# Who issues the copies that begin the sums of the MLP's weights: the load queue, job by job, or GpSimd, several jobs interleaved

## The chip, the cores and the metric

The kernel runs on 1 core of one Trainium2 chip. The metric is the device time of one execution, in microseconds; the number given for a kernel is the median of several runs. The profile is one execution more, taken by the hardware profiler. "Load queue" is SyncE's DMA queue (SP). ScalarE (ACT) and GpSimd (POOL) have a queue each as well.

## The reference, cut to what matters

One layer of a decoder over 2048 tokens of width 1024, all in float32: retention and a pooling mixer, cross-attention into 256 memory tokens, then a gated MLP with a short causal convolution. Two parts matter here: the cross-attention, whose key side starts from the *normalised* memory, and the MLP.

```python
mem_n = rmsnorm(mem, mem_norm_g)
...
q = (h @ wq).reshape(B, S, XA_HEADS, XA_HEAD_DIM)
k, v = jnp.split(mem_n @ wkv, 2, axis=-1)
...
a = h @ w_up                      # 1024 -> 2 x 2816
c = conv_w[0] * a2 + conv_w[1] * a1 + conv_w[2] * a + conv_b
gate, val = jnp.split(c, 2, axis=-1)
return (jax.nn.silu(gate) * val) @ w_down
```

## The kernel before, in words

**Arithmetic.** Each float32 operand is split into a high part that fits TensorE's fast format and a low part, and each product is three matmuls (high by high, high by low, low by high: lines 241, 242, 243, in `passes`). ScalarE makes the high parts, VectorE the low parts (lines 233 and 216).

**The start (`folded_weights`, and `load_x_wide` beside it).** The 16 projections of the memory (`project(n)`, `wkv[n]`, 24 matmuls of 128x256 each) run on the memory without its norm, and the first eight results are multiplied by the norm's factors as they leave PSUM. The factors come from `memory_norm`: ScalarE squares the two halves of the memory (L389), GpSimd adds the squares in five `tensor_tensor` instructions (L216 on POOL), TensorE sums over partitions (L317, tile `aux3`), VectorE takes the inverse root, TensorE spreads it over the partitions (L341, tile `aux9`), ScalarE copies it out (L346). PSUM has five buffers for products (pool `mmp`), so the first five projections (tiles mm1, mm2, mm10, mm11, mm12) can be computed before one has left; the sixth (mm13) needs a buffer back. The memory's two raw tiles lie in arena `Z` and are given back once GpSimd has added them; the loads of x and of the value weights (L540, L659) take the places in `Z` in turn.

**The weights' sums.** The MLP multiplies 2x2 blocks with seven products in place of eight, and for that needs four sums of blocks of each weight: with blocks a11, a12, a21, a22 they are d2 = a21 + a22, d0 = a11 + a21, d1 = a11 + d2 and d3 = a12 + d1. `weight_sums` makes them from DRAM to DRAM, without any engine: four plain copies begin the sums (one block each), then four DMAs with `accum_op=add` finish them. There are 34 jobs, 22 for `w_up` into `Ud` and 12 for `w_dn` into `Dd`; a block is 256 KB (192 KB in four of the jobs). Before the change the copies are issued by SP (L917) and held with `issue_after` behind the last load of a tile that the program has fetched; the accumulating DMAs are issued by POOL (L919, L920, L923, L926). Only GpSimd's queue can accumulate. The sums are read from 1,126 us on, for the MLP.

**What sets the order.** `weight_sums` is a generator kept in `under[0]`; the program takes a step of it now and then (in `unit`, between quarters of a projection, and in `attention`, `pace` steps for each of 16 tiles of rows, `pace` being 1 in the first block of rows and 2 in the second). Whatever is left runs ahead of the MLP. The written order isn't the final one: a scheduler places the instructions of the five engines, by a timeline of its own, and moves an instruction ahead of the place where it was written when its operands allow it. In the finished program each engine goes through its own list strictly in order and waits at an instruction until its semaphores are there. The DMAs of POOL share eight semaphores in turn, so from the ninth on each waits for the one issued eight before it; those of SP and ACT share eight likewise.

Of the kernel before, what the change touches and what calls it, by code (L numbers as in the profile page):

```python
# [12 lines left out]
ALU = mybir.AluOpType  # L13
# [106 lines left out]
def trunk(ctx, tc, xT, memT, pos, w_qkgu, w_v, wkv, wqT, wo, wout_r, wout_p, poolT, w_up, w_dn, vecs, consts, outT):  # L120
    nc = tc.nc
    pe, act, dve, pool, sp = nc.tensor, nc.scalar, nc.vector, nc.gpsimd, nc.sync
# [15 lines left out]
    def new_z(dtype):  # L138
        return Arena(cp.tile([P, 8 * T + 4 * EDGE], dtype, tag="Z", name=nm("Z")), 0, 8, T)
# [58 lines left out]
    def mmps():  # L198
        return mmp.tile([P, SUB], F32, tag="mm", name=nm("mm"))
# [6 lines left out]
    def aux():  # L206
        if both[0] and next(turns_) % 3 == 2:
            return single()
        return auxp.tile([P, SUB], F32, tag="aux", name=nm("aux"))

    def small(n=4):
        t = smp.tile([P, 8], F32, tag="sm", name=nm("sm"))
        return t[:, :n]

    def tt(eng, out, a, b, op):
        return eng.tensor_tensor(out=out, in0=a, in1=b, op=op)  # L216

    def ts(eng, out, a, s1, op0, s2=None, op1=None):
        if op1 is None:
            eng.tensor_scalar(out=out, in0=a, scalar1=s1, scalar2=None, op0=op0)  # L220
        else:
            eng.tensor_scalar(out=out, in0=a, scalar1=s1, scalar2=s2, op0=op0, op1=op1)
# [7 lines left out]
    def split(src, hi, lo, g=None):  # L230

        if g is None:
            act.activation(hi, src, AF.Copy)  # L233
            tt(dve, lo, src, hi.bitcast(F32), ALU.subtract)
        else:
            act.activation(hi, src, AF.Identity, scale=g)
            stt(lo, src, g, hi.bitcast(F32), ALU.mult, ALU.subtract)

    def passes(ps, lhs, rhs, start, stop, more=False):
        (lh, ll), (rh, rl) = lhs, rhs  # L240
        pe.matmul(ps, lh, rh, start=start, stop=False, skip_group_check=more)  # L241
        pe.matmul(ps, lh, rl, start=False, stop=False, skip_group_check=more)  # L242
        latest[0] = pe.matmul(ps, ll, rh, start=False, stop=stop, skip_group_check=more)  # L243

    def new_raw():
        r = raws.take()
        r.free()
        return r.f
# [6 lines left out]
    def pairs(raw):  # L255

        out = []
        for h in range(2):
            r = raw[h] if isinstance(raw, list) else raw[:, h * SUB : (h + 1) * SUB]
            pr = new_pair()  # L260
            split(r, pr[:, 0], pr[:, 1])
            out.append(pr)
        return out
# [15 lines left out]
    behind, under, fetched = [iter(())], [iter(())], [None]  # L279
# [544 lines left out]
    def attention(sums, beside, pace):  # L824


        scl, nscl = (smp.tile([P, 8], F32, tag="scl", name=nm("scl"), bufs=2) for _ in range(2))
        room = B.take(2 * KT)
        third = [Region(B, room.first + KT * i, KT) for i in range(2)] + [new_z(F32R).take(KT)]
        prob = [third[1], third[0]]  # L830

        def load_m(hp):

            out = mw[hp]
            for kp in range(KT // 2):
                raw = new_raw()
                fetched[0] = sp.dma_start(raw.rearrange("p (k n) -> p k n", k=2), Md[hp, 2 * kp : 2 * kp + 2].rearrange("k p n -> p k n"))
                if hp == 0 and kp == 0:

                    out += [(pr[:, 0], pr[:, 1]) for pr in pairs(raw)]  # L840
                    yield
                    continue
                for i in range(2):
                    u = third[2 * hp].r[:, (2 * kp + i) * T : (2 * kp + i + 1) * T]
                    split(raw[:, i * SUB : (i + 1) * SUB], u[:, :SUB], u[:, SUB:])
                    out.append((u[:, :SUB], u[:, SUB:]))
                yield

        def turn(pt, t, e):
            tp = aux()  # L850
            for j in range(4):
                pe.transpose(tp[:, j * P : (j + 1) * P], e.f[:, j * P : (j + 1) * P], ident)  # L852
            pt4 = pt.r.rearrange("p (i k t) -> p i k t", i=2, t=T)[:, :, :, t * P : (t + 1) * P]
            turned.append(act.activation(pt4[:, 0], tp.rearrange("p (k t) -> p k t", k=4), AF.Copy))
            tt(dve, pt4[:, 1], tp.rearrange("p (k t) -> p k t", k=4), pt4[:, 0].bitcast(F32), ALU.subtract)
            e.free()

        turned.clear()
        mw = [[], []]
        for _ in load_m(0):  # L860
            pass
        more_m = load_m(1)
        late = []
        for i in range(2 * KT):
            hp, t = divmod(i, KT)
            ps = mmps()
            for k in range(KT):
                x2 = [X[:, 2 * k + j, t * P : (t + 1) * P] for j in range(2)]
                passes(ps, x2, mw[hp][k], k == 0, k == KT - 1)
            if i == 0:  # L870
                rn, _, _ = norm_tables(sums, wide=False)
                ts(dve, scl, rn, 1.0 / 16.0, ALU.mult)
                ts(dve, nscl, rn, -1.0 / 16.0, ALU.mult)
            mx, sm = small(2), small(2)
            dve.reduce_max(out=mx, in_=ps.rearrange("p (h m) -> p h m", h=2), axis=AX.X)
            ts(dve, mx, mx, nscl[:, t : t + 1], ALU.mult)
            e = TT.take()
            for j in range(2):
                act.activation(e.f[:, j * NMEM : (j + 1) * NMEM], ps[:, j * NMEM : (j + 1) * NMEM], AF.Exp,
                               bias=mx[:, j : j + 1], scale=scl[:, t : t + 1], accum_out=sm[:, j : j + 1])  # L880
            dve.reciprocal(sm, sm)
            for j in range(2):
                ej = e.f[:, j * NMEM : (j + 1) * NMEM]
                ts(dve, ej, ej, sm[:, j : j + 1], ALU.mult)
            if len(late) == 2:
                turn(*late.pop(0))
            late.append((prob[hp], t, e))
            for _ in range(pace):
                next(under[0], None)
            if i < KT - 2:  # L890
                next(more_m, None)
            else:
                for _ in range(pace):
                    next(beside, None)

        def end():
            for one in late:
                yield turn(*one)

        return prob, end()  # L900


    def block(w, g, h, k0, n):

        return w[g][:, k0 + h * n : k0 + (h + 1) * n].rearrange("p k c -> p (k c)")

    def weight_sums():

        jobs = [((w_up[f], w_up[f + NF]), 0, 4, Ud[f]) for f in range(NF)]
        for at, (k0, n) in enumerate(ROUNDS):  # L910
            jobs += [((w_dn[2 * j], w_dn[2 * j + 1]), k0, n, Dd[at, j]) for j in range(KT // 2)]
        for w, k0, n, to, in jobs:
            a11, a12, a21, a22 = (block(w, i // 2, i % 2, k0, n) for i in range(4))
            d = [to[i][:, : n * P] for i in range(4)]
            with tc.issue_after(fetched[0].ins):
                for i, a in ((2, a21), (0, a11), (1, a11), (3, a12)):
                    sp.dma_start(d[i], a)  # L917
            yield
            pool.dma_start(d[2], a22, accum_op=ALU.add, max_dma_last_dim=2048)  # L919
            pool.dma_start(d[0], a21, accum_op=ALU.add, max_dma_last_dim=2048)  # L920
            yield
            yield
            pool.dma_start(d[1], d[2], accum_op=ALU.add, max_dma_last_dim=2048)  # L923
            yield
            yield
            pool.dma_start(d[3], d[1], accum_op=ALU.add, max_dma_last_dim=2048)  # L926

    class Round:

# [409 lines left out]
    pending, later, sums, Y, fetches, firsts = [], [], [], [], [], []  # L1339
# [113 lines left out]
    def norm_tables(s_acc, wide=True, late=False):  # L1453

        rn = rows_norm(s_acc)
        rb, last = [], None
        if wide:
            rb = [TT.take() for _ in range(NS)]
            last = spread(rn, [r.f[:, :SUB] for r in rb], late=late)
        return rn, rb, last  # L1460
# [68 lines left out]
    normed = norm_tables(room[:1])  # L1529
    wv.append(value_weights(3, Z.take()))  # L1530
    under[0] = weight_sums()
    for b in range(NB):

# [49 lines left out]

        beside = tables() if b + 1 < NB else first_tiles(own)
        prob, behind[0] = attention(xs, beside, b + 1)
        for _ in beside:
            pass
# [181 lines left out]
```

## Time and profile before

| | |
|---|---|
| Time, 3 runs | 2470.78 us median (2470.77 to 2472.31) |
| The profiled execution | 2470.94 us, of which its span 2469.2 us |
| Granted TensorE clock, mean | 0.996 |
| Busy share: PE, PEld, DVE, ACT, POOL | 98%, 82%, 69%, 49%, 7% |
| DMA queues, MB: SP's, POOL's, ACT's | 409.23, 34.61, 28.32 |
| DMAs of the sums: SP's copies; POOL's accumulations | 136; 136 |
| POOL's first and last DMA of the sums, issued at | 47.66 us, 921.23 us |

How to read it: the span runs from the first to the last instruction. A waits view lists, for an engine and a line, what ended the idle time ahead of it. A windows view gives the busy time of each engine in stretches of the span. A timeline has the start of an instruction, its duration, what it writes and reads, and in brackets the idle time ahead of it. The order of an engine's list (not from a trace) has no times in it.

### The profile page before, as it was taken

How to read it: one execution, taken by the hardware profiler on the slowest of the kernel's cores; microseconds unless marked ns; L12 is line 12 of the kernel's file. 1: busy time of each engine (PE TensorE's matmuls, PEld its weight loads, DVE VectorE, ACT ScalarE, POOL GpSimd, SP SyncE). 2: the span in 40 equal slices, each digit the busy share in tenths (PEclk: the TensorE clock that was granted, in tenths of full speed). 3: DMA queues.
4: the chain of work that ended last, by engine and by line, in shares of the span. 5: the costliest groups of instructions: out<-in, count | busy, mean ns of one | idle time of the engine just before them, and what ended most of it. 6: DMA issues, size and time to landing. Idle time of an engine off the chain costs nothing.

```text
span 2469.2 us, 33010 instructions
## 1 busy us (share of the span) xinstructions
PE 2430.5 (98%) x11390; PEld 2032.3 (82%) x11390; DVE 1706.8 (69%) x2913; ACT 1219.9 (49%) x2170; POOL 182.9 (7%) x240
## 2 busy tenths in 40 slices
PE   6999999999999999999999999999999999999997
PEld 6888888888888888888888888888888888888886
DVE  8646576564636574575679776896767688867875
ACT  6333423443421223434655555665555577666663
POOL 1010121100021110000000100020000000000000
PEclk9999999999999999999999999999999999999998
DMA  9363889726676674366568655765457479768951
GB/s 321 91 167 116 233 198 246 230 49 196 189 189 154 152 160 147 111 223 223 156 205 275 208 182 156 229 211 174 154 158 217 135 228 309 238 189 281 345 169 68
DMA packets 257176, 474.27 MB, mean 192 GB/s; under 512 B 26864, under 2 KB 56176, under 8 KB 257008
## 3 DMA queue, kind: packets, MB, share of 16 engines
q1 hardware_dynamic: 212912, 409.23, 50.7%
q0 software_dynamic: 19584, 34.61, 9.2%
q10 hardware_dynamic: 24512, 28.32, 3.3%
q8 instruction: 89, 1.46, 0.2%
q14 instruction: 79, 0.65, 0.1%
HBM read 370.87 MB, written 170.39 MB: 219 GB/s over the span
## 4 chain that ended last, share of the span: by engine, by line
PE 95%; DVE 2%; DMA 1%; ACT 1%; issue 0%; POOLq 0%; POOL 0%; SPq 0%; ACTq 0%; DVEq 0%
PE mm L241 30%; PE mm L243 30%; PE mm L242 30%; PE aux L751 1%; PE aux L852 1%; PE aux L764 1%; PE aux L740 1%; PE aux L766 1%; PE aux L243 1%; PE aux L242 1%; PE aux L241 1%; PE aux L317 1%; DVE Z L216 0%; DMA R<-wo 0%; DMA Z<-xT 0%
## 5 line engine op out<-in xcount | busy, mean ns | idle before, releaser
L241 PE MATMUL mm<-G,Q 128*128 128x512 f32 (+1 forms) x1888 | 726.2, 385 | 17.2 <-ACT Q L233 11.3
L243 PE MATMUL mm<-G,Q 128*128 128x512 f32 (+1 forms) x1888 | 724.7, 385 | 4.6 <-DVE Q L216 4.4
L242 PE MATMUL mm<-G,Q 128*128 128x512 f32 (+1 forms) x1888 | 723.8, 384 | 0.0
L242 PE MATMUL mm<-G 128*128 128x512 f32 (+1 forms) x1380 | 530.0, 384 | 0.0
L241 PE MATMUL mm<-G 128*128 128x512 f32 (+1 forms) x1380 | 528.3, 385 | 0.4 <-ACT T L474 0.4
L243 PE MATMUL mm<-G 128*128 128x512 f32 (+1 forms) x1380 | 528.2, 385 | 0.0
L241 PEld LDWEIGHTS mm<-G,Q 128*128 128x128 f32 x1888 | 357.0, 189 | 85.8 <-ACT Q L233 11.9
L243 PEld LDWEIGHTS mm<-G,Q 128*128 128x128 f32 x1888 | 356.6, 189 | 73.7 <-DVE Q L216 5.7
L242 PEld LDWEIGHTS mm<-G,Q 128*128 128x128 f32 x1888 | 357.0, 189 | 67.9 <-DVE G L216 0.4
L241 PEld LDWEIGHTS mm<-G 128*128 128x128 f32 x1380 | 259.3, 188 | 51.9 <-ACT T L474 0.6
L242 PEld LDWEIGHTS mm<-G 128*128 128x128 f32 x1380 | 259.3, 188 | 51.4
L243 PEld LDWEIGHTS mm<-G 128*128 128x128 f32 x1380 | 259.3, 188 | 51.3
L1008 ACT ACTIVATE G<-R 128x512 fp32r<-128x512 f32 (+1 forms) x272 | 167.2, 616 | 251.9 <-PE mm L242 243.4
L216 DVE TENSOR_TENSOR Q<-R,Q 128x512 fp32r<-128x512 f32 x235 | 162.5, 694 | 151.3 <-ACT Q L233 136.8
L216 DVE TENSOR_TENSOR Z<-Z,mm 128x512 f32<-128x512 f32 x284 | 193.9, 683 | 101.8 <-PE mm L243 101.6
L225 DVE SCALAR_TENSOR_TENSOR Z<-Z,vecs 128x1024 f32<-128x1024 f32 x176 | 224.7, 1281 | 50.4 <-ACT Z L1071 45.8
L216 DVE TENSOR_TENSOR G<-R,G 128x512 fp32r<-128x512 f32 (+1 forms) x268 | 178.6, 675 | 109.7 <-ACT G L1008 70.7
L233 ACT ACTIVATE Q<-R 128x512 fp32r<-128x512 f32 x150 | 93.6, 628 | 243.1 <-PE mm L242 221.4
L1008 ACT ACTIVATE Q<-R 128x512 fp32r<-128x512 f32 (+1 forms) x204 | 125.5, 615 | 98.0 <-PE mm L242 80.6
L216 DVE TENSOR_TENSOR G<-T,G 128x512 fp32r<-128x512 f32 (+1 forms) x201 | 133.0, 677 | 45.0 <-ACT G L957 31.0
L216 DVE TENSOR_TENSOR T<-T 128x512 f32<-128x512 f32 (+3 forms) x218 | 149.3, 689 | 18.0 <-ACT T L357 9.7
L1071 ACT ACTIVATE Z<-Z,vecs 128x1024 f32<-128x1024 f32 x88 | 109.1, 1241 | 33.0 <-DVE Z L216 32.1
(216 smaller groups left out, 2480.9 us busy)
## 6 DMA issues: line engine op xcount, KB each, us to landing
R<-Ud SPq DMA_DIRECT2D x176, 256.0 KB, 2.8
T<-Gd SPq DMA_DIRECT2D x168, 256.0 KB, 4.4
R<-w_up SPq DMA_DIRECT2D x132, 256.0 KB, 3.2
Gd<-Z SPq DMA_DIRECT2D x110, 256.0 KB, 2.8
Ud<-w_up SPq DMA_DIRECT2D x88, 256.0 KB, 6.3
R<-w_qkgu SPq DMA_DIRECT2D x32, 512.0 KB, 4.5
R<-Dd SPq DMA_DIRECT2D x64, 256.0 KB, 4.4
Gd<-T SPq DMA_DIRECT2D x56, 256.0 KB, 3.5
```

Of the source, the lines that this page charges most:

```text
L216: return eng.tensor_tensor(out=out, in0=a, in1=b, op=op)
L225: dve.scalar_tensor_tensor(out=out, in0=a, scalar=s, in1=b, op0=op0, op1=op1)
L233: act.activation(hi, src, AF.Copy)
L241: pe.matmul(ps, lh, rh, start=start, stop=False, skip_group_check=more)
L242: pe.matmul(ps, lh, rl, start=False, stop=False, skip_group_check=more)
L243: latest[0] = pe.matmul(ps, ll, rh, start=False, stop=stop, skip_group_check=more)
L317: pe.matmul(ps[:, t : t + 1], ap, one, start=True, stop=more is None)
L740: pe.matmul(col(sc, c), self.ch(k, c), self.ch(q, c), start=True, stop=True)
L751: pe.matmul(col(self.kv, c), col(self.kn.f, c), self.ch(v, c, h * T), start=True, stop=True)
L764: pe.matmul(col(y, c), col(self.pr.f, c), self.ch(v, c, h * T), start=True, stop=self.cur[c] is None)
L1008: act.activation(p2[:, 0, :w], self.raw[i].f[:, :w], AF.Copy)
L1071: act.activation(self.c[g].f, a[:, 2:], AF.Identity, bias=cb[:, f : f + 1], scale=cw[2][:, f : f + 1])
```

## The change: what it does

```diff
-            for _ in range(pace):
+            for _ in range(4 - pace):
                 next(under[0], None)
...
-        for w, k0, n, to, in jobs:
+
+        def sums(w, k0, n, to):
             a11, a12, a21, a22 = (block(w, i // 2, i % 2, k0, n) for i in range(4))
             d = [to[i][:, : n * P] for i in range(4)]
-            with tc.issue_after(fetched[0].ins):
-                for i, a in ((2, a21), (0, a11), (1, a11), (3, a12)):
-                    sp.dma_start(d[i], a)
+
+            def add(at, a):
+                pool.dma_start(d[at], a, accum_op=ALU.add, max_dma_last_dim=2048)
+
+            for i, a in ((2, a21), (0, a11), (1, a11), (3, a12)):
+                pool.dma_start(d[i], a, max_dma_last_dim=2048)
             yield
-            pool.dma_start(d[2], a22, accum_op=ALU.add, max_dma_last_dim=2048)
-            pool.dma_start(d[0], a21, accum_op=ALU.add, max_dma_last_dim=2048)
+            add(2, a22)
+            add(0, a21)
             yield
+            add(1, d[2])
             yield
-            pool.dma_start(d[1], d[2], accum_op=ALU.add, max_dma_last_dim=2048)
-            yield
-            yield
-            pool.dma_start(d[3], d[1], accum_op=ALU.add, max_dma_last_dim=2048)
+            add(3, d[1])
+
+        live, jobs = [], [sums(*j) for j in jobs]
+        while jobs or live:
+            if jobs:
+                live.append(jobs.pop(0))
+            for g in list(live):
+                if next(g, True) is not None:
+                    live.remove(g)
+                yield
```

The 136 copies move from SP's list to POOL's (now L921; the accumulations are L918), up to four jobs are under way at once, and beside the attention 3 and 2 steps are taken for a tile in place of 1 and 2. The `issue_after` that held the copies is gone with them: a copy has no operand that any engine makes. The lists of the engines differ between the two programs up to about row 2,230 of 10,729 on PE; behind that they are the same but for line numbers.

On POOL, before, the list begins with the memory norm's five additions (`Z_73` is the arena with the memory's raw tiles, `T` the sum), and the first accumulation of the first job follows them:

```order
L1765 UNCONDITIONAL_BRANCH
L216 ISA
L216 TENSOR_TENSOR Z_73<-Z_73 128x512
L216 TENSOR_TENSOR T<-Z_73 128x256
L216 TENSOR_TENSOR Z_73<-Z_73 128x512
L216 TENSOR_TENSOR Z_73<-Z_73 128x256
L216 TENSOR_TENSOR T<-T,Z_73 128x256
L919 DMA Ud<-w_up 128x512
```

On POOL, after, 16 copies, one accumulation and one more copy stand ahead of the first of the five additions:

```order
L1776 UNCONDITIONAL_BRANCH
L921 DMA Ud<-w_up 128x512 x16
L918 DMA Ud<-w_up 128x512
L921 DMA Ud<-w_up 128x512
L216 ISA
L216 TENSOR_TENSOR Z_73<-Z_73 128x512
```

The additions two to four follow among further DMAs, and this is the place of the fifth, which completes the sum that L317 reads:

```order
L216 TENSOR_TENSOR Z_73<-Z_73 128x256
L921 DMA Ud<-w_up 128x512
L918 DMA Ud<-w_up 128x512
L921 DMA Ud<-w_up 128x512
L918 DMA Ud<-w_up 128x512
L921 DMA Ud<-w_up 128x512 x4
L918 DMA Ud<-w_up 128x512 x2
L921 DMA Ud<-w_up 128x512 x3
L216 TENSOR_TENSOR T<-T,Z_73 128x256
L918 DMA Ud<-Ud 128x512
```

Counted over the whole list, the five additions stood behind no DMA; now they stand behind 18, 21, 30, 33 and 46 DMAs, and of the 46 ahead of the fifth 38 are copies and 8 accumulations.

On PE, before, the norm's sum over partitions (`aux3`) stands behind the second projection (mm2) and ahead of the third (mm10):

```order
L242 MATMUL mm2_151<-G_72,Q_76 128x256
L243 MATMUL mm2_151<-G_72,Q_76 128x256
L317 MATMUL aux3_183<-consts_78,T_74 128x1 x2
L241 MATMUL mm10_222<-G_72,Q_76 128x256
L242 MATMUL mm10_222<-G_72,Q_76 128x256
```

On PE, after, the same sum stands behind the fifth projection (mm12), directly ahead of the spreading (`aux9`) and of the sixth projection (mm13):

```order
L242 MATMUL mm12_288<-G_72,Q_76 128x256
L243 MATMUL mm12_288<-G_72,Q_76 128x256
L317 MATMUL aux3_183<-consts_78,T_74 128x1 x2
L341 MATMUL aux9_205<-G_72,ones_92 128x256 x2
L241 MATMUL mm13_321<-G_72,Q_76 128x256
L242 MATMUL mm13_321<-G_72,Q_76 128x256
```

The sum has moved back past three projections.

On SP, after, two loads of x wait for POOL to give back the memory's raw tiles (rows with what they wait for; DMAHW are SP's own eight semaphores):

```order
L659 DMA Z_73<-w_v 128x2x512 [waits DMAHW5_49,DVE_49]
L540 DMA Z_73<-xT 128x1024 [waits DMAHW6_49,Pool_49]
L659 DMA Z_73<-w_v 128x2x512 [waits DMAHW7_49,DVE_49]
L540 DMA Z_73<-xT 128x1024 [waits DMAHW0_49,Pool_49]
L659 DMA Z_73<-w_v 128x2x512 [waits DMAHW5_49,DMAHW1_49,DVE_49]
L413 DMA T<-wkv 128x512 [waits DMAHW2_49,PE_49]
```

Before, these two waits were there as well, further ahead in the list (the third and the fifth load of x); now they are at the sixth and the seventh.

## The prediction

> **What bounds the kernel now.** I read the page first (who is busy, and the chain that ended last), then the busy time by stage, then TensorE's waits, then the start, instruction by instruction. The page:
>
> ```profile
> span 2469.2 us, 33010 instructions
> PE 2430.5 (98%) x11390; PEld 2032.3 (82%) x11390; DVE 1706.8 (69%) x2913; ACT 1219.9 (49%) x2170; POOL 182.9 (7%) x240
> PE 95%; DVE 2%; DMA 1%; ACT 1%; issue 0%; POOLq 0%; POOL 0%; SPq 0%; ACTq 0%; DVEq 0%
> ```
>
> TensorE is busy 2430.5 of 2469.2 us, so only 38.7 us are idle on it. The change touches none of its instructions, only what they wait for: it can win a part of 38.7 us, and can lose without a bound. Where the idle time lies, by stage (start and end, length, then busy time of PE, PEld, DVE, ACT and POOL, granted clock, DMA share, GB/s):
>
> ```profile
> 0.00:62.00 62.00, 41.41 (x291) 39.43 (x291) 54.19 (x94) 42.36 (x65) 9.47 (x12) 0.94 0.92 320
> 62.00:262.00 200.00, 198.19 (x1095) 172.09 (x1095) 117.88 (x242) 74.57 (x160) 10.58 (x13) 1.00 0.46 124
> 262.00:580.00 318.00, 318.00 (x1519) 265.67 (x1518) 195.94 (x425) 122.24 (x259) 40.11 (x48) 1.00 0.71 195
> 580.00:923.00 343.00, 343.00 (x1689) 289.63 (x1688) 203.01 (x436) 92.60 (x200) 59.25 (x72) 1.00 0.71 172
> 923.00:1235.00 312.00, 311.14 (x1416) 257.11 (x1416) 189.07 (x339) 133.94 (x258) 1.95 (x8) 1.00 0.52 172
> 1235.00:2440.00 1205.00, 1204.67 (x5322) 997.49 (x5321) 927.59 (x1329) 747.82 (x1221) 57.77 (x84) 1.00 0.65 208
> 2440.00:2469.20 29.20, 14.08 (x69) 10.90 (x67) 19.16 (x51) 6.39 (x10) 3.72 (x3) 0.77 0.39 144
> ```
>
> 20.6 us of it are in the first 62 us, 15.1 in the last 29, and from 62 to 2440 us, where the sums are made and used, only 3.0. In the first 62 us the DMA engines are 92% busy: the start is the one stage in which they are short. TensorE's waits say the same by their ends:
>
> ```profile
> PE mm L241 <- ACT Q L233: 11.3, 4, 9.1
> PE mm L241 <- DVE T L216: 4.7, 1, 4.7
> PE mm L243 <- DVE Q L216: 4.4, 4, 2.1
> ```
>
> 9.1 us is the wait for the first tile. The 4.7 us is the wait of the sixth projection for a PSUM buffer, which the norm of the memory must release. That chain in the timeline, GpSimd's additions first, then TensorE's three steps:
>
> ```profile
> 8.61 1.65 POOL L216 TENSOR_TENSOR Z<-Z 128x512 f32<-128x512 f32 x1 [8.16 <-ACT Z L389]
> 10.33 1.06 POOL L216 TENSOR_TENSOR T<-Z 128x256 f32<-128x256 f32 x1
> ...
> 15.50 1.07 POOL L216 TENSOR_TENSOR T<-T,Z 128x256 f32<-128x256 f32 x1
> ```
>
> ```profile
> 18.96 0.50 PE L317 MATMUL aux<-consts,T 128*128 128x1 f32 x4
> 28.04 0.40 PE L341 MATMUL aux<-G,ones 128*128 128x256 f32 x2
> 33.15 0.58 PE L241 MATMUL mm<-G,Q 128*128 128x256 f32 x1 [4.71 <-DVE T L216]
> ```
>
> The additions end at 16.57 us, and the sixth projection starts at 33.15. So **the memory's norm already sets when TensorE goes on**, and it runs through GpSimd's list.
>
> **The change, part by part.** *The copies leave SP, and `pace` changes.* What the step of the generator costs at its written place doesn't count, since the copies now stand at the head of POOL's list; SP gains 136 issues of room, at a cost of nothing to TensorE except where one of them delayed a load. All the mid-run idle time (3.0 us) is the ceiling of that.
>
> *Forty-six DMAs stand ahead of the fifth addition.* What POOL pays to issue them is seen where it issued five in a row:
>
> ```profile
> 693.71 0.81 POOL L923 DMA_DIRECT2D Ud<-Ud  x1 [8.06 <-DMA Ud<-w_up]
> 694.24 1.12 POOL L919 DMA_DIRECT2D Ud<-w_up  x1
> 694.76 1.44 POOL L920 DMA_DIRECT2D Ud<-w_up  x1
> 695.29 1.75 POOL L919 DMA_DIRECT2D Ud<-w_up  x1
> 695.82 2.10 POOL L920 DMA_DIRECT2D Ud<-w_up  x1
> ```
>
> Starts and durations together end at 694.52, 695.36, 696.20, 697.04 and 697.92: one every 0.84 us. So 46 x 0.84 = 38.6 us is the least, and the fifth addition can't start before about 40 us in place of 15.50. The other limit is that only eight of POOL's DMAs can be under way: the 46th can be issued once the 38th has landed, so 38 blocks must have gone through DMA engines that the loads keep busy. The queues' rows (packets, MB, share of the 16 engines' time) of the first 62 us, of 690 to 696.5 us, and of 703 to 708 us:
>
> ```profile
> q1 hardware_dynamic: 7615, 19.02, 84.0%
> ```
>
> ```profile
> q1 hardware_dynamic: 770, 1.58, 65.8%
> q0 software_dynamic: 263, 0.47, 40.9%
> ```
>
> ```profile
> q0 software_dynamic: 611, 1.00, 113.5%
> ```
>
> SP's queue (q1) moved 19.02 MB in 0.84 x 62 = 52.1 us of the engines, 365 GB/s. In the second window, where it was mostly copies of the sums, 1.58 MB took 0.658 x 6.5 = 4.28 us: 369 GB/s, or 0.71 us for a block of 0.262 MB. In the third, POOL's queue (q0) had the engines to itself and accumulated 1.00 MB in 5 us: 1.31 us for a block. A *plain copy on POOL's queue* is in no row of before: its bounds are 0.71 us (the same copy on SP's queue) and 1.31 us (an accumulation, which reads twice); I take 0.71, the row of the same bytes and accesses, and keep 1.31 for the range. Of the first 38 DMAs, 32 are copies and 6 accumulations: 32 x 0.71 + 6 x 1.31 = 30.6 us of all 16 engines.
>
> Against them run SP's loads. Ahead of the load of x that waits for the fifth addition, SP's list has 22 loads of 0.524 MB, the constants and the vectors, 12.0 MB in all, 32.9 us at 365 GB/s. Both amounts have to pass unless one queue gets much the better of the other: 30.6 + 32.9 = 63.5 us, and with the first DMA at about 1.5 us the fifth addition starts at 65 us. In the second window above POOL's queue got 40.9% of the engines; at that, SP's part is through at 32.9 / 0.59 = 56 us, POOL having done 23 of its 30.6 us by then, and the rest takes it to the same 64.
>
> The Trainium skill ("DMA: Bandwidth & Descriptors", section "Queues, rings and completion order") says that each DMA engine takes turns between the queues packet by packet; the 40.9% against 65.8% agree with it roughly, and with equal turns the 30.6 us would need 61 us, so the sum would come out at 62 in place of 65.
>
> From the addition to the sixth projection TensorE took 14.2 us from L317, but most of that was VectorE busy with other tiles. The links alone: 0.54 to VectorE, 13 tiny steps 2.1 (19.50 to 24.23, less 2.66 for three tiles between them), one split of x 1.28 and the diagonals 1.15 between, the spread 0.40, ScalarE's copy 0.36, the first multiplication out of PSUM 0.42, plus the tiles that stand ahead of it in VectorE's list:
>
> ```profile
> 19.50 0.16 DVE L222 TENSOR_SCALAR sm<-aux 128x2 f32<-128x2 f32 x1 [0.55 <-PE aux L317]
> 24.06 0.17 DVE L397 COPY rnm<-sm 128x2 f32<-128x2 f32 x1
> 26.67 0.42 DVE L216 TENSOR_TENSOR G<-consts,yh 128x256 fp32r<-128x256 f32 x1
> 30.11 0.36 ACT L346 ACTIVATE T<-aux 128x256 f32<-128x256 f32 x1
> 32.67 1.74 DVE L216 TENSOR_TENSOR T<-mm,T 128x256 f32<-128x256 f32 x5
> ```
>
> I take 8 us behind the addition's end at 66: the sixth projection at **74 us in place of 33.15, +41 us**. The five projections ahead don't help: they were done at 28 us before, and even with loads at 60% of their rate are done by about 40, so TensorE then stands idle at L317.
>
> *What is late next.* SP stands at the load of x until the fifth addition; behind it wait the value weights, the last wkv tiles and the first w_qkgu: 19.02 - 12.0 - 1.05 (four copies) = 6 MB, at 59% of 365 GB/s 28 us, from 66 to 94. TensorE's own work of this stretch (41.41 us less the 17.3 up to L341) is 24 us, from 74 to 98. The two fit, so of the 4.7 us of further waits that 33 to 62 us held about 2 go: **-2** (bounds -4.7 and +8, if the loads run 28 us after a start that lags).
>
> *Contention behind the start.* POOL has 226 DMAs left then, some 98 x 0.71 + 128 x 1.31 = 237 us of the engines, which it now pours out as fast as eight at a time allow. The nearest rows are those of 330 to 420 us of before (the stage, then the queues' shares):
>
> ```profile
> 330.00:420.00 90.00, 90.00 (x438) 75.83 (x437) 63.07 (x142) 26.73 (x57) 19.10 (x23) 1.00 0.93 240
> ```
>
> ```profile
> q1 hardware_dynamic: 7152, 13.06, 43.9%
> q0 software_dynamic: 3170, 5.77, 40.2%
> ```
>
> The engines were 93% busy there, 40% for POOL's queue, and TensorE lost nothing (90.00 of 90.00). The folding of the weights, 62 to 262 us, has shorter leads (1.8 us lost even at 46%). I take **+4** for it, with 0 and +15 as bounds: four loads and stores on its chain, each some 4 us later at most. **The sum: +41 - 2 + 4 = +43 us on the profiled execution's 2470.9 us, 2514 us;** that execution is 0.2 us from the runs' median, so the same number stands for it.
>
> **The rivals.** (1) *POOL's queue gets the better of SP's.* If the loads' packets give way, only issuing bounds: the fifth addition at 40 us, the sixth projection at 49, +16, and the loads that SP couldn't make take back the 4.7: about +12, 2483 us. For it: a copy is short, and eight are always waiting. Against it: the 40.9%. (2) *Copies on POOL's queue cost as much as accumulations.* Then 38 x 1.31 + 32.9 = 82.7, the addition at 84, +60, and with the upper bound of the contention +75, 2546 us. For it: every row of q0 is slower by the byte than any of q1. Against it: those rows read twice. (3) *Faster: SP, rid of the copies, loads sooner, and the additions aren't held.* That is decided by when the fifth addition ends: up to about 25 us the sixth projection still starts at 33. Then the waits of 33 to 62 us (4.7) and the mid-run ones of 62 to 1235 us (2.7) may go, 2463.5 us. For it: four copies did stand ahead of loads for the arena `Z`:
>
> ```profile
> 41.76 2.54 SPq L917 DMA_DIRECT2D Ud<-w_up  x4
> 44.72 0.39 SPq L659 DMA_DIRECT2D Z<-w_v  x1
> 46.45 0.34 SPq L540 DMA_DIRECT2D Z<-xT  x1
> ```
>
> Against it: 46 DMAs would have to be issued in 24 us, 0.52 us each, while the rows above show 0.84. (4) *GpSimd is locked out while VectorE works*, so that issuing gets several times dearer:
>
> ```profile
> L923 POOL DMA_DIRECT2D Ud<-Ud x8: 812/818/840, 301.2 to 416.5; - x8
> ```
>
> With five times 0.81 the 46 issues would take 187 us, the sixth projection would start near 196, +163, 2634 us. The row speaks against it: 812 to 840 ns between 301 and 417 us, with VectorE busy 62% of that stage. The Trainium skill ("SBUF — State Buffer", section "SBUF: two separate sides") warns of it for DMAs issued by GpSimd, beside VectorE's faster modes, with 620 ns grown to 3,100; no row here shows it.
>
> **How the numbers follow.** My forecast (2495 to 2535) gets 0.66, rival (1) 0.14, (2) 0.13, (3) 0.03, (4) 0.01, and 0.03 is left for a hold that TensorE hardly notices, within 0.2%, which is about what a measurement of this kernel can tell from no change. The range takes in (1) and (2): 2483 to 2546. By sign: faster 0.03, the same 0.03, slower 0.94.
>
> **What would show it right or wrong.** In the profile after, the fifth addition on POOL at 55 to 75 us, with DMAs and waits for their landing ahead of it; TensorE idle at L317 for 20 to 35 us and then waiting for the multiplications out of PSUM; SP idle at L540 until that addition; the first 62 us of DMA at 95% or more with q0 above a third; POOL's DMAs finished long before 921 us; from about 600 us on nothing changed. The fifth addition before 30 us, or TensorE's loss outside the first 110 us, would make the prediction wrong.

## The result, and the profile after

The changed kernel takes **2558.16 us** (median of 5 runs, 2552.97 to 2560.81), the kernel before 2472.31 us in 5 runs: a ratio of 1.0343, 95% interval [1.0326, 1.0361]. The change costs about 86 us, where 43 were forecast, and the time lies above the range. The page of the changed kernel (span, busy time, and the chain that ended last, by engine and by line):

```profile
span 2559.0 us, 32883 instructions
PE 2446.1 (96%) x11390; PEld 2043.1 (80%) x11390; DVE 1708.0 (67%) x2913; ACT 1222.1 (48%) x2170; POOL 252.7 (10%) x376
PE 89%; DMA 4%; DVE 1%; ACT 1%; ACTq 1%; issue 0%; POOLq 0%; SPq 0%; POOL 0%; DVEq 0%
```

The profiled execution is the longest of the five (2560.81 us); its span grew by 89.8 us, where the median grew by 86. TensorE's idle time is 2559.0 - 2446.1 = 112.9 us, against 38.7 before: +74.2. The other 15.6 us are busy time: the same 11,390 matmuls took 2446.1 us in place of 2430.5. By stage (start and end, length, then busy time of PE, PEld, DVE, ACT and POOL, granted clock, DMA share, GB/s), first after, then the last two of these stages before:

```profile
0.00:62.00 62.00, 19.64 (x120) 18.43 (x120) 25.27 (x34) 24.81 (x31) 30.32 (x52) 0.79 1.00 359
62.00:262.00 200.00, 187.91 (x1067) 166.37 (x1068) 123.39 (x241) 77.62 (x153) 104.54 (x150) 0.94 1.07 282
262.00:380.00 118.00, 75.78 (x346) 60.92 (x345) 38.79 (x83) 31.47 (x67) 56.70 (x79) 0.86 1.10 279
380.00:668.00 288.00, 288.00 (x1370) 240.86 (x1369) 181.15 (x403) 106.88 (x233) 0.00 (x0) 0.99 0.31 107
```

```profile
262.00:380.00 118.00, 118.00 (x600) 100.16 (x599) 74.39 (x174) 40.10 (x92) 21.50 (x26) 1.00 0.88 226
380.00:668.00 288.00, 288.00 (x1317) 238.66 (x1316) 170.39 (x340) 119.62 (x231) 25.21 (x30) 1.00 0.62 179
```

The loss lies in two places: at the start, which the forecast named and whose hold runs on to 72.8 us, into the second stage, and from 262 to 380 us, where 42 of 118 us are idle and before not one was. The granted clock of these stages is lower too (0.79, 0.94 and 0.86, against 0.94, 1.00 and 1.00), and matmuls are slower at a lower clock. In two stretches of 4 us without a gap, just behind the hold and a little later, TensorE goes through 19 matmuls of 128x256 at 0.50 and 36 at 1.00:

```profile
73.00:77.00 4.00, 4.00 (x19) 4.00 (x20) 3.44 (x10) 2.16 (x6) 1.78 (x3) 0.50 1.08 331
78.00:82.00 4.00, 4.00 (x36) 4.00 (x35) 3.09 (x6) 2.69 (x6) 1.84 (x4) 1.00 1.10 297
```

By the trace's clock records TensorE was busy for 29 us at half speed, against 7 before; half of the difference, 11 us, is most of the 15.6 us (an estimate). From 380 us on POOL has no sums left, and nothing is lost. TensorE's waits after (total, times, longest, in us):

```profile
PE aux L317 <- POOL T L216: 31.8, 1, 31.8
PE aux L751 <- ACT T L746: 20.6, 3, 17.8
PE mm L241 <- DVE T L216: 14.2, 2, 12.1
...
PE mm L241 <- ACT T L492: 9.0, 5, 2.6
```

The first row is the norm's addition. The second and the last wait for ScalarE at L746 and L492, and 12.1 us of the third for VectorE at L216; together they are 41.7 of the 42.2 us that are idle from 262 to 380 us. Each of these instructions needs a tile `T` to write to, and the chain that ended last says why the tiles were not there (start, length, what):

```profile
259.74 15.63 DMA Md<-T
...
320.63 24.72 DMA VWd<-T
...
355.24 23.06 DMA VWd<-T
378.32 0.69 ACT T L746
```

These are stores: `keep` (L434) writes folded weights from a tile `T` to DRAM on ACT's queue, and the tile is free again once the store has landed. A store of 256 KB of `VWd` took 23 to 25 us there.

Where the delay grows is seen best by how much later the same instruction of TensorE starts than before. Four such points: the first matmul of the sixth projection (33.15 us before); the first transpose at L742 (168.19), in the retention, which TensorE does between the parts of the folding; and the fourth and the last of the eight groups of transposes at L779, in the retention too (259.86 and 374.02). The lists of TensorE are not in the same order in all the kernels, so the points are taken where as much work stands ahead: 126 matmuls at the first, 862 at the second, 1,372 or 1,378 at the third (in e8 1,402), 1,950 to 1,957 at the fourth. The stores of `Md` are issued from 145 to 223 us before, half of them behind the second point; those of `VWd` from 252 to 289 us. So the third of the four intervals has the later stores of `Md`, and the last has `VWd`. For the changed kernel and all experiments, in us:

| kernel | 6th projection | L742 | 4th group | 8th group | span |
|---|---|---|---|---|---|
| the change | +39.7 | +39.9 | +48.6 | +87.8 | +89.8 |
| e1, copies behind the norm | +0.9 | +3.4 | +14.3 | +62.2 | +60.7 |
| e2, norm on VectorE | +7.4 | +27.7 | +44.1 | +85.8 | +85.1 |
| e3, `VWd` in wide rows | +41.2 | +39.9 | +49.4 | +56.6 | +57.0 |
| e4, e1 and e3 together | +0.3 | +6.2 | +17.0 | +42.9 | +42.7 |
| e5, only the queue changed | +38.9 | +36.2 | +45.1 | +89.8 | +91.4 |
| e6, all but the queue changed | +0.4 | -0.3 | -1.2 | -0.1 | +21.9 |
| e7, before, with the hold alone | +40.2 | +35.3 | +35.5 | +35.4 | +38.2 |
| e8, copies paced | +0.3 | +2.6 | +18.3 | +19.8 | +35.4 |
| e9, stores issued by SP | +38.1 | +39.1 | +54.9 | +84.4 | +84.5 |
| e10, e4 and `WPd` in wide rows | +0.5 | +3.0 | +14.6 | +26.1 | +25.0 |

So the change loses 39.7 us up to the sixth projection, next to nothing from there to L742, 8.7 up to the fourth group, 39 over the stretch with `VWd`'s stores, and 2 in all the rest.

### The profile page after: what moved, and what is told of

It reads as the page before. It is cut to its first block, busy times and chain, and to the rows that moved or that the text cites. A ratio compares the mean times of both kernels' runs of the same rounds, so it can differ in the third digit from the quotient of the medians.

```text
span 2559.0 us, 32883 instructions
## 1 busy us (share of the span) xinstructions
PE 2446.1 (96%) x11390; PEld 2043.1 (80%) x11390; DVE 1708.0 (67%) x2913; ACT 1222.1 (48%) x2170; POOL 252.7 (10%) x376
## 3 DMA queue, kind: packets, MB, share of 16 engines
q1 hardware_dynamic: 193328, 374.62, 44.1%
## 4 chain that ended last, share of the span: by engine, by line
PE 89%; DMA 4%; DVE 1%; ACT 1%; ACTq 1%; issue 0%; POOLq 0%; SPq 0%; POOL 0%; DVEq 0%
PE mm L241 28%; PE mm L243 28%; PE mm L242 28%; DMA VWd<-T 2%; DMA Md<-T 1%; DMA T<-Xd 1%; PE aux L751 1%; PE aux L764 1%; PE aux L740 1%; PE aux L766 1%; ACTq L434 1%; PE aux L317 1%; DMA Hd<-T 1%; PE aux L243 0%; PE aux L242 0%; PE aux L241 0%
## 5 line engine op out<-in xcount | busy, mean ns | idle before, releaser
L241 PE MATMUL mm<-G 128*128 128x512 f32 (+1 forms) x1380 | 529.6, 386 | 15.5 <-DVE T L216 12.1
L216 DVE TENSOR_TENSOR Q<-R,Q 128x512 fp32r<-128x512 f32 x235 | 162.3, 693 | 180.2 <-ACT Q L233 165.7
L216 DVE TENSOR_TENSOR G<-R,G 128x512 fp32r<-128x512 f32 (+1 forms) x268 | 177.9, 673 | 130.0 <-ACT G L1019 74.1
L216 DVE TENSOR_TENSOR Z<-Z,mm 128x512 f32<-128x512 f32 x284 | 193.3, 681 | 106.1 <-PE mm L243 105.7
L216 DVE TENSOR_TENSOR G<-T,G 128x512 fp32r<-128x512 f32 (+1 forms) x201 | 132.8, 675 | 44.6 <-ACT G L968 30.8
L216 DVE TENSOR_TENSOR T<-T 128x512 f32<-128x512 f32 (+3 forms) x218 | 149.0, 688 | 19.1 <-ACT T L357 10.0
```

## The experiments

The theory after the result: the start is lost to the additions held on GpSimd, and the stretch from 260 to 380 us to `VWd`'s stores, which are written in pieces of 512 bytes and lose against POOL's queue, now never empty. The rivals: the start is lost to the shared DMA engines whatever is held; any store is late while the engines are full; it isn't the stores' landing but the issuing on ACT; and it is the interleaving, not the queue.

**e1: the copies behind the norm.** The copies may be issued only behind the fifth addition.

```diff
-                    tt(pool, s_m.f[:, :NMEM], s_m.f[:, :NMEM], f[:, :NMEM], ALU.add)
+                    normed_mem[0] = tt(pool, s_m.f[:, :NMEM], s_m.f[:, :NMEM], f[:, :NMEM], ALU.add)
...
-            for i, a in ((2, a21), (0, a11), (1, a11), (3, a12)):
-                pool.dma_start(d[i], a, max_dma_last_dim=2048)
+            with tc.issue_after(normed_mem[0].ins):
+                for i, a in ((2, a21), (0, a11), (1, a11), (3, a12)):
+                    pool.dma_start(d[i], a, max_dma_last_dim=2048)
```

> The changed kernel, but POOL's first copies are held behind the memory norm's fifth addition, so that the five additions stand ahead of all DMAs of the sums. Theory (two separate costs, the held norm about 40 us, the stores of the folded weights starved by POOL's queue about 45 us): the sixth projection starts at 33 to 40 us, the loads from 17 us on are slowed by up to 12 us, the second cost stays, in all 2515 to 2535 us. Rival (POOL's bytes have to pass the DMA engines anyway, and TensorE waits for them one way or the other): within 10 us of 2558.

Measured: 2536.22 us (2532.0 to 2540.43), ratio 1.0253 [1.0209, 1.0297], 1 us above the range of the theory. The sixth projection is back at 34.0 us, and up to L742 3.4 us are lost in place of 39.9. But between the fourth and the eighth group 48 us are lost, more than in the change, and the gain of 36 at the start shrinks to 29 in the span (23 between the medians, each against its own runs of before). TensorE's waits in the whole run, and the stores of `VWd` from 262 to 380 us (KB each, median us from issue to landing):

```profile
PE mm L241 <- DVE T L216: 22.5, 5, 7.9
...
PE aux L752 <- ACT T L747: 10.4, 3, 7.2
```

```profile
VWd<-T ACTq DMA_DIRECT2D x16, 256.0 KB, 25.2
```

So the larger loss doesn't hang on the late start: it is there with the start mended, when the stores still meet the sums.

**e2: the norm on VectorE.** The five additions leave GpSimd; its DMAs run from 1 us on, as in the change.

```diff
-                tt(pool, f[:, :SUB], f[:, :SUB], f[:, SUB:], ALU.add)
+                tt(dve, f[:, :SUB], f[:, :SUB], f[:, SUB:], ALU.add)
...
-                    tt(pool, s_m.f[:, :NMEM], s_m.f[:, :NMEM], f[:, :NMEM], ALU.add)
+                    tt(dve, s_m.f[:, :NMEM], s_m.f[:, :NMEM], f[:, :NMEM], ALU.add)
```

> The changed kernel, with the memory norm's five additions on VectorE in place of POOL; POOL's DMAs start at 1 us as in the changed kernel. Theory: the hold goes while the DMA engines are shared from the first microsecond on, so the sixth projection starts at 36 to 48 us and the whole takes 2518 to 2540 us. Rival (the start is lost to shared DMA engines, not to POOL's list): the sixth projection stays at 65 us or later and the whole at 2550 to 2560.

Measured: 2557.59 us (2556.08 to 2559.09), ratio 1.0339 [1.0309, 1.0369]. **A miss for the theory, which had it at 2518 to 2540.** The hold is gone (sixth projection at 40.51 us), yet 27.7 us are lost up to L742, and 44.1 up to the fourth group, nearly as many as in the change (48.6). The first two stages, TensorE's waits, and the queues' shares of the first 62 us:

```profile
0.00:62.00 62.00, 37.98 (x241) 36.09 (x242) 40.78 (x82) 31.57 (x48) 26.53 (x50) 0.90 1.00 358
62.00:262.00 200.00, 182.45 (x970) 158.53 (x969) 108.49 (x201) 69.84 (x138) 105.07 (x152) 0.94 1.08 289
```

```profile
PE mm L241 <- ACT Q L233: 17.9, 6, 9.2
...
PE mm L242 <- DVE G L216: 6.7, 3, 5.6
```

```profile
q1 hardware_dynamic: 4202, 11.65, 50.0%
q0 software_dynamic: 3512, 10.50, 49.5%
```

By 262 us TensorE has done 1,211 matmuls, against 1,386 before, with no wait over 10 us: it is fed by splits (`Q`, `G`) of tiles that SP loaded, and SP moved 11.65 MB in the first 62 us where 19.02 had been moved before. The start is bounded twice, by the held addition and by the loads that give half the engines away, and taking one away leaves most of the other. In e1, where POOL's first copy is issued at 16.3 us, SP moves 14.62 MB in the first 62 us and only 3.4 us are lost up to L742; by these two runs the sharing costs most in the first 16 us.

**e7: the hold alone.** The kernel before, with 32 additions of no use ahead of the fifth on GpSimd, so that it ends as late as in the change, with no DMA moved.

```diff
-                    tt(pool, s_m.f[:, :NMEM], s_m.f[:, :NMEM], f[:, :NMEM], ALU.add)
+                    for _ in range(32):
+                        busy = tt(pool, f[:, SUB:], f[:, SUB:], f[:, SUB:], ALU.add)
+                    with tc.issue_after(busy.ins):
+                        tt(pool, s_m.f[:, :NMEM], s_m.f[:, :NMEM], f[:, :NMEM], ALU.add)
```

> The kernel before, with 32 further additions on POOL (128x512, on a part of the memory's tile that is no longer needed, some 1.46 us each) ahead of the memory norm's fifth addition, and nothing of the sums moved: the hold without the DMAs. Theory (the hold costs by itself what the start lost): the fifth addition at about 62 us, the sixth projection at 70 to 73, in all 2506 to 2518 us. Rival (the start is lost to the shared DMA engines, and a hold alone is largely caught up, since all loads are there when it ends): under 2495.

Measured: 2509.5 us (2509.17 to 2509.82), ratio 1.0139 [1.0118, 1.0159]; in the trace +40.2 at the sixth projection, +35.3 at L742, and the same from there to 374 us. So the hold by itself is worth some 35 us and gives a few of its 40 back behind it, and with no backlog nothing is lost at `VWd`'s stores.

**e3: wide rows for `VWd`.** The tensor in DRAM is laid out so that a store writes rows of 2 KB in place of 512-byte pieces; the loads of it take the small pieces instead, later.

```diff
-    VWd = drp.tile([KT, P, KT, P], F32, tag="VWd", name="VWd")
+    VWd = drp.tile([2, KT, P, SUB], F32, tag="VWd", name="VWd")
...
-                    keep(tiles4(VWd, nh, 2 * h + mt), t, 4)
+                    act.dma_start(VWd[nh, 2 * h + mt], t.f[:, :SUB])
+                    t.free()
...
```

> The changed kernel, with the product of the value projection and wo (VWd) laid out in DRAM so that the 16 stores write rows of 2 KB in place of pieces of 512 bytes; the 16 loads of it then read pieces of 512 bytes, at a time when POOL issues nothing. Theory (turns by piece: a store of 512-byte pieces gets a quarter of the bytes of 2-KB pieces for each turn): the stores land in under 12 us in place of 23, TensorE's loss between 290 and 385 us falls from some 40 to under 15 us, in all 2525 to 2538 us. Rival (the bytes of POOL's queue, or the issuing on ACT, whatever the pieces): 2550 to 2560.

Measured: 2528.94 us (2528.22 to 2529.66), ratio 1.0223 [1.0194, 1.0253]. The loss between the fourth and the eighth group falls from 39.2 to 7.2 us. The queues from 298 to 380 us (packets, MB, share of the engines' time) and the stores, in the change and then in e3:

```profile
q0 software_dynamic: 6975, 14.51, 78.7%
q10 hardware_dynamic: 8315, 4.13, 20.8%
...
VWd<-T ACTq DMA_DIRECT2D x16, 256.0 KB, 20.5
```

```profile
q0 software_dynamic: 6610, 13.79, 75.0%
...
q10 hardware_dynamic: 2596, 4.34, 15.1%
...
VWd<-T ACTq DMA_DIRECT2D x16, 256.0 KB, 8.6
```

The same megabytes on ACT's queue (q10), nearly the same backlog on POOL's (q0), but a third of the packets: the landing falls from 20.5 to 8.6 us. That is the size of the pieces, and not only full engines.

**e4 and e10: e1 with wide rows.** e4 joins the edits of e1 and e3; e10 lays `WPd`, a store of the same kind, in wide rows as well.

```diff
-    WPd = drp.tile([KT, P, 4, P], F32, tag="WPd", name="WPd")
+    WPd = drp.tile([2, 4, P, SUB], F32, tag="WPd", name="WPd")
...
-                keep(tiles4(WPd, nh, g), t, 4)
+                act.dma_start(WPd[nh, g], t.f[:, :SUB])
+                t.free()
...
```

> Both edits of the two kernels with the norm first and with wide rows. Theory, if the two costs add: 2482 to 2505 us. Rival (the second cost is there only because the first moved the stores): the same as with the norm first alone, within 5 us.

> As e4 (the copies behind the fifth addition, VWd in rows of 2 KB), and WPd in rows of 2 KB too. Theory, small pieces lose against the sums' backlog wherever they are stored: in e4 TensorE still waited 7.2 and 10.1 us at the lines behind WPd's stores, so some 10 to 17 us come back, 2496 to 2504. Rival, the 16 engines are full there (109% of their span) and any store is late: within 4 us of e4, 2509 to 2518.

Measured: e4 2513.43 us (2513.24 to 2513.61), ratio 1.0161 [1.0131, 1.019]. **A miss**: it lies 8 us above the theory and far below the rival, so the two gains do not simply add. e10 2495.92 us (2493.58 to 2496.84), ratio 1.0086 [1.0069, 1.0103], 0.1 us below the theory's range. In e4 the sums still run at 390 us, and `WPd`'s stores (335 to 381 us) meet them, which in the change (404 to 422 us) they do not. TensorE's waits there in e4, then what is left of the same wait in e10:

```profile
PE aux L768 <- DVE T L758: 10.1, 1, 10.1
...
PE aux L753 <- ACT T L748: 7.2, 3, 4.3
```

```profile
PE aux L769 <- DVE T L759: 3.7, 1, 3.7
...
PE aux L754 <- ACT T L749: 2.7, 2, 1.4
```

10.9 of 17.3 us went, and the time fell by 17.5. The size of the pieces counts in another tensor too.

**e9: the stores issued by SP.** In the change ACT stood still at some of `VWd`'s issues (start and duration; 0.37 us is usual):

```profile
313.85 6.01 ACTq L434 DMA_DIRECT2D VWd<-T  x1
...
320.63 4.16 ACTq L434 DMA_DIRECT2D VWd<-T  x1
...
326.59 4.52 ACTq L434 DMA_DIRECT2D VWd<-T  x1
```

```diff
-            act.dma_start(dst, t.f[:, :SUB].rearrange("p (n c) -> p n c", n=n))
+            sp.dma_start(dst, t.f[:, :SUB].rearrange("p (n c) -> p n c", n=n))
```

> The change, but the folding's and the projections' stores to DRAM (Md, VWd, WPd) are issued by the load queue, SP, in place of ACT; pieces of 512 bytes as before. In the change ACT's queue stood still in front of VWd's stores for some 27 us in all between 298 and 371 us (nine issues of 0.5 to 6.0 us where 0.37 is usual). Theory A, the blocked issue is what delays TensorE there, since the evictions queued behind it on ACT come late: 20 to 27 us come back, 2530 to 2540. Theory B, the late landing is what delays it, since the tiles that the stores read are not free before the bytes have landed, whoever issues them: within 8 us of the change, 2550 to 2566. Were SP's loads blocked behind the stores instead, it would be above 2566.

Measured: 2556.28 us (2554.14 to 2557.48), ratio 1.0331 [1.0316, 1.0347]: the same as the change. SP now stands still at the issues (shortest, median and longest duration in ns, first and last start), and the chain goes through a store all the same:

```profile
L434 SPq DMA_DIRECT2D VWd<-T x16: 359/592/5498, 304.8 to 373.4; - x16
```

```profile
326.88 27.54 DMA VWd<-T
```

So the total doesn't hang on the engine that issues. By stretches it is less clean: between the fourth and the eighth group 29 us are lost in place of 39, and between L742 and the fourth 16 in place of 9. SP's own loads now stand behind the stores, so one standstill may have taken the place of another: up to 10 of the 39 us may be ACT's standing still, and no run here separates that from the landing.

**e5: only the queue.** The kernel before, job by job and at its own pace; the copies alone go to GpSimd, with the `issue_after` left around them.

```diff
-                    sp.dma_start(d[i], a)
+                    pool.dma_start(d[i], a, max_dma_last_dim=2048)
```

> The kernel before, with only the copies' queue changed (POOL in place of SP, the issue_after around them kept); jobs one after another and the pace beside the attention as before. Theory (the queue is all of it, since issue_after orders only within one engine's list and so no longer holds the copies): within 12 us of the changed kernel, 2546 to 2570. Rival (the interleaving of four jobs or the larger pace makes the backlog): under 2500.

Measured: 2562.22 us (2561.8 to 2562.64), ratio 1.0352 [1.0331, 1.0372]. The queue is the whole of it: without the interleaving and without the pace, the loss is the same within 4 us at every point of the table. On GpSimd the `issue_after` held nothing back: the first eight copies stand at 1.27 us here and at 1.28 in the change.

**e6: all but the queue.** The change, with the copies on SP again behind the last fetched load.

```diff
-            for i, a in ((2, a21), (0, a11), (1, a11), (3, a12)):
-                pool.dma_start(d[i], a, max_dma_last_dim=2048)
+            with tc.issue_after(fetched[0].ins):
+                for i, a in ((2, a21), (0, a11), (1, a11), (3, a12)):
+                    sp.dma_start(d[i], a)
```

> The changed kernel with its copies given back to SP, behind the last load, as before; the interleaving of jobs and the larger pace stay. Theory: within 5 us of the kernel before, 2468 to 2478. Rival (interleaving and pace carry part of the loss): 2485 or more.

Measured: 2496.08 us (2491.62 to 2499.49), ratio 1.0083 [1.0065, 1.0102]. **A miss**: the interleaving and the larger pace were held to cost nothing, and cost 21 us. Nothing is lost up to 374 us. Then the sums, taken up faster, fill 380 to 668 us (POOL's queue and SP's copies at once), and a load of x lands late, with ScalarE's list behind it and TensorE at L852 behind that (the stage; TensorE's wait; the chain):

```profile
380.00:668.00 288.00, 273.27 (x1218) 225.71 (x1217) 158.33 (x309) 106.02 (x210) 61.02 (x73) 0.96 0.88 235
```

```profile
PE aux L852 <- DVE T L220: 12.2, 2, 11.9
```

```profile
532.34 18.97 DMA T<-xT
```

Before, the DMA engines were 62% busy in this stage and TensorE lost nothing. Whether it is the interleaving or the pace was not tried apart.

**e8: the copies paced.** They stay on GpSimd, but each job's copies wait for VectorE to have reached the place where the program takes the step (a flag that VectorE writes and GpSimd reads).

```diff
...
+            j = next(ticks)
+            with tc.issue_after(low_part[0].ins):
+                dve.memset(halo[:, j, 0:1], 0.0)
+            held = pool.tensor_copy(halo[:, j, 1:2], halo[:, j, 0:1])
+            with tc.issue_after(held.ins):
```

> The changed kernel, with each job's copies on POOL behind a tiny POOL copy that waits for a tiny VectorE write, and that write stands in VectorE's list behind the low part that was made last when the step is taken: POOL's list then follows VectorE's progress, and the memory norm's additions stand ahead of all copies. Theory (the loss is a backlog on POOL, of 46 DMAs at the start and of eight in flight throughout): the sums end after 600 us, both losses go, 2468 to 2482 us. Rival (plain copies on POOL's queue cost time wherever they are): 2490 or more.

Measured: 2504.84 us (2499.74 to 2507.1), ratio 1.0114 [1.0095, 1.0132]. **A miss** for the theory that pacing gives all of it back. The start is mended (+2.6 at L742), and `VWd`'s stretch for the most part. The fourth group has 30 more matmuls ahead of it here, some 6 us of work at 0.2 us each (an estimate); without them about 10 us are lost up to it, where `Md`'s stores meet a burst of sums, and about 7 from there to the eighth. 15.6 more are lost behind 374 us, where loads of x land late as in e6; the last sums are issued at 794 us, not by 600. The chain at two of these places:

```profile
231.32 10.86 DMA Md<-T
...
615.27 15.46 DMA T<-xT
```

No kernel here beats the one before; of those with the copies on GpSimd e10 comes nearest.

## Why the prediction was half right

**The direction, the hold and its sum were right.** POOL's additions, the load of x behind them on SP, and TensorE's three steps, after:

```profile
1.28 4.36 POOL L921 DMA_DIRECT2D Ud<-w_up  x8 [0.83 <-POOLq L1772]
...
63.64 0.73 POOL L216 TENSOR_TENSOR T<-T,Z 128x256 f32<-128x256 f32 x1
```

```profile
64.40 0.33 SPq L540 DMA_DIRECT2D Z<-xT  x1
```

```profile
64.43 1.02 PE L317 MATMUL aux<-consts,T 128*128 128x1 f32 x4 [31.76 <-POOL T L216]
...
72.81 0.58 PE L241 MATMUL mm<-G,Q 128*128 128x256 f32 x1 [2.09 <-DVE T L216]
```

The fifth addition is at 63.64 us (65 forecast), the sixth projection at 72.81 (74), the hold at L317 31.8 us (20 to 35).

**Its parts.** A plain copy on POOL's queue, unknown before, cost what the near row said: at 1.31 us a block the sum has the addition at 84 us, and it came at 63.64. The *issuing* was taken too dear: eight copies in 4.36 us, 0.55 each in place of 0.84. That changed nothing, since landing was what bound. POOL's *share* of the engines was not 40.9% but half; the 40.9% are of a window, 690 to 696.5 us, in which POOL issued nothing before 693.71:

```profile
q0 software_dynamic: 3607, 10.58, 50.7%
q1 hardware_dynamic: 4306, 11.66, 49.0%
```

Rival (1) needed loads that give way entirely, which half and half is not. (2), copies at the price of accumulations, falls with the addition's place, and so does (3): what was held against (3), 0.84 us for an issue, was wrong, but landing keeps the addition back all the same. (4) falls with the 0.55 us.

**"The rest of the start, -2"** was wrong by a little and in its reasoning by more. It gave nothing back: the delay was 39.7 us at the sixth projection and 39.9 at L742 (168.19 us before, 208.08 after). e7 shows that the hold alone would have given 5 of it back up to there (35.3 left); e2 shows that the shared loads alone come to 27.7. The text put them in a row, as hold and slack; they are two limits that run side by side, 35.3 and 27.7 us singly and 39.9 together.

**The step that failed is "contention behind the start, +4, with 0 and +15 as bounds".** From L742 on it measured +8.7 up to the fourth group, and +39.2 from there to the eighth: 48 us. Two things were wrong in it. The row that carried it, 330 to 420 us of before with the engines 93% busy and no loss, was of a stretch whose traffic is mostly the sums themselves (47 blocks) and loads; the stores of `VWd` had ended by then, and only three of `WPd`'s were left. And "four loads and stores, each some 4 us later at most" had neither their number (16 of `VWd` alone) nor what one costs. Before, from 250 to 300 us:

```profile
q10 hardware_dynamic: 8448, 4.20, 28.6%
q0 software_dynamic: 738, 1.36, 17.8%
...
VWd<-T ACTq DMA_DIRECT2D x16, 256.0 KB, 5.5
```

These rows would have allowed the sum. 4.20 MB in 8,448 packets are 500 bytes each, so a packet of the profile is one piece. A packet of q0 holds an engine 0.178 x 50 x 16 / 738 = 0.193 us, one of q10 0.286 x 50 x 16 / 8448 = 0.027 us. If the two queues pass pieces one for one, a store of 512 pieces, 32 for each engine, needs 32 x 0.22 = 7.0 us, an estimate; from the change's rows (298 to 380 us: 0.148 and 0.033 us) it is 5.8. Sixteen stores need 93 to 113 us so, where before they were issued within 37; they were issued within 73 (298.5 to 371.2 us) and delayed TensorE by 39. Where these two queues have the engines to themselves in the change, from 352 to 370 us, their packets do come out even:

```profile
q0 software_dynamic: 1633, 2.98, 89.6%
q10 hardware_dynamic: 1636, 0.81, 22.2%
```

512 pieces for each 5.6 us, and 3.7 times as many bytes for POOL. The Trainium skill ("DMA: Bandwidth & Descriptors", section "Queues, rings and completion order") has each engine take turns between its queues by packets, which it says typically hold some 9 to 17 descriptors. The equal counts agree with turns of as many pieces for either queue; how many pieces go in one turn, no run here shows.

The prediction's own test, "TensorE's loss outside the first 110 us would make the prediction wrong", is what caught it. The 15.6 us of longer busy time, most of it the lower clock, were in no term at all. That nothing changes from 600 us on held nearly: +87.8 us at the eighth group, at 374 us of before, and +89.8 at the end.

**What stays open**: the last 22 us of e10 (25 in its trace), of which the table puts 3 up to L742, 12 from there to the fourth group and 11 from the fourth to the eighth. The 12 lie where `Md`'s later stores meet the sums, and every kernel whose sums run there loses 9 to 16 us in that interval; `Md`, in pieces of 1 KB, was not widened, so its part is argued and not shown. Open are also ACT's part of `VWd`'s 39 us (e9), and which part of e6's 21 us is interleaving and which is pace.

## What to carry to other kernels

When background DMAs are moved to a queue on which nothing holds them, look for every store whose source buffer is waited for, count its pieces, and price each piece together with one packet of the other queue. "The engines were as busy elsewhere and nothing was lost" is no evidence unless the same kind of transfer was made there. An ordering that worked on one engine's list (`issue_after` behind a load on SP) may hold nothing on another's, and two limits that run side by side must each be taken away, singly and jointly, before either is given the whole loss.

## What the runs showed of the hardware

- GpSimd issued plain DRAM-to-DRAM copies of 256 KB every 0.55 us (eight in 4.36 us), accumulating ones in 0.81 to 0.84 us.
- With both queues full in the first 62 us, POOL's and SP's had half the engines each (50.7% and 49.0%; 49.5% and 50.0% in e2).
- POOL's and ACT's queues passed as many packets as each other from 352 to 370 us of the change (1,633 and 1,636), of 1.8 KB and of 0.5 KB on average.
- Behind POOL's backlog an engine stood still while it issued a store: up to 6.01 us on ACT in the change, up to 5.50 us on SP in e9, where 0.37 us is usual.
- TensorE's granted clock was lower in stages with idle gaps (0.79 in the first 62 us and 0.86 from 262 to 380 us, against 0.94 and 1.00): 4 us without a gap held 19 matmuls of 128x256 at 0.50 and 36 at 1.00.
